# Moving weight copies and accumulating transfers between the stages of an fp32 encoder layer

## The chip, the cores and the metric

The kernel runs on one core of a Trainium2 chip. The core's engines have a queue each: TensorE (PE; its weight loads are listed as PEld), VectorE (DVE), ScalarE (ACT), GpSimd (POOL) and SyncE (SP), which here only issues DMAs. An engine works its queue in order: an instruction that waits holds all behind it. Sixteen DMA engines move the data that SyncE, GpSimd and ScalarE ask for. The metric is the device time of one execution in microseconds, smaller is better.

## The reference

One layer of a streaming encoder, batch 1, 512 positions, width 1024, everything in float32:

```python
hn = rmsnorm(h, norm_mix_g)
fq, fk, fv, ff, gq, gf, gi, gg = split(hn @ w_in)      # 1024 -> 3 x 512 + 8 + 4 x 512
fox_out = forgetting_attention(fq, fk, fv, log_sigmoid(ff + fox_f_bias))   # 8 heads of 64
rec = hgrn2_chunkwise(gq, gf, gi, lbs)                 # 4 heads, state 128 x 128
rec = rmsnorm(rec, hgrn_norm_g) * silu(gg)
h = h + concat([fox_out, rec]) @ w_out                 # 1024 -> 1024
mem_n = rmsnorm(mem, norm_mem_g)                       # 256 memory rows
h = h + cross_attention(rmsnorm(h, norm_x_g), mem_n, w_xq, w_xkv, w_xo)    # 4 heads of 256
u = rmsnorm(h, norm_ff_g) @ w1                         # 1024 -> 4096
h = h + square(relu(u)) @ w2                           # 4096 -> 1024
return rmsnorm(h, final_norm_g)
```

## The kernel before

**Products.** Each float32 operand is split into a high part in a shorter format and the low rest, and each product is made as three matmuls (high by high, high by low, low by high). A weight block comes from memory as a raw tile (`wr`); ScalarE copies it into the high part (`wh`, L181), VectorE subtracts that from the raw tile into the low part (`wl`, L185). The helper `split_of` emits the two.

**Panels.** `specs` lists 38 weight panels of 1 MB in the order of their use: 0 to 12 and 15 from `w_in` (gates, recurrence, the attention's projections), 13, 14 and 16 to 21 from `w_xkv` (values, then keys of the memory), 22 to 25 `w_out`, 26 to 29 `w_xq`, 30 to 33 `w_xo`, 34 to 37 the first two groups of `w1`. `next_panel` hands out a panel and first sees that the one behind it is asked for. `load_next` loads a panel in two halves, a and b (19b is the second half of panel 19), each through `load_unit`: new high and low tiles (four buffers of each, so two panels), a raw tile, the DMAs on SyncE (L205), and the split. Raw tiles come from a pool with two buffers. From panel `LATE` on every third half takes its raw tile from another pool, `t4`, with one buffer, which before that holds the query and key rows (`qk`) of the attention's four projections. `len(stream)` is the number of the panel that is loaded.

**MLP by sums.** The MLP has eight groups of 512 hidden units. For six of the up products and all eight of the down products the 2 x 2 block matrices are multiplied by seven products instead of eight (a Strassen scheme), for which four sums of weight blocks are needed in each case: "5", "7", "6", "4". They are made in memory, ahead of time: `first` copies a block from `w1` or `w2` into a scratch tensor (`wsu` or `wsd`, L433, SyncE, memory to memory, 512 KB), and a later DMA from GpSimd adds another block to it (L443). "6" adds the finished "5" and "4" the finished "6". There are 14 such sets, so 56 copies and 56 accumulations. The deque `copies` holds the copies in pairs of sets (d0 and u2, d1 and u3, and so on; d is down, u is up, the number is the group). In the MLP the sums are loaded as raw tiles (`wrd`, `wru`, L1327) like plain blocks.

**When copies and accumulations are issued.** A copy is issued behind the DMA of a half panel, in program order on SyncE, from panel `COPIES` on, one for each half. An accumulation is issued by `Presum.tick`. Each group of three matmuls reports the time that it should take, and the sum of that, `spent`, is the kernel's own clock; where it passes `self.next`, the next accumulation is emitted and made to wait for the matmul that reported. `PACE` gives the spacing: pairs of a beginning and a gap, and a gap of `None` skips to the next beginning. The clock counts only these matmuls: 183 of it is reached at 271.5 us, 307.2 at 435.6 us.

**Stages and order.** First comes the projection of the gates (panels 0 to 3), then the recurrence over levels 1, 2, 4 to 64 (L797 on TensorE, L803, L822 and L823 on VectorE and GpSimd, mixes on ScalarE), with the projections of panels 4 to 10 filled in between (the class `Fill`). Then come the recurrence's output, and the forgetting attention with panels 10 to 21 as its filling: scores (L1020), softmax (L1031 to L1035), transposes (`pt`, L1043), output (L1059). The stages after it are `w_out`, the cross attention, `w_xo` and the MLP. TensorE's order is that of the program. ScalarE, VectorE, GpSimd and SyncE are ordered by the framework's planner, by its own costs and with priorities (`ahead`), except in a few stretches that are marked as written by hand.

Of the kernel before, what the change touches and what calls it, by code (L numbers as in the profile page):

```python
# [38 lines left out]
NEG = -3.0e38  # L39
SEVEN = (2, 3, 4, 5, 6, 7)  # L40
RAWS, HB, LOADS = 6, 4, 8
COPIES = 3
PACE = (25.0, 9.0), (97.0, None), (183.0, 4.6), (306.0, 9.5)


@with_exitstack
def emit(
# [58 lines left out]
    def t4(name):  # L106
        return t4p.tile([P, D], F32, tag="t4", name=name)
# [25 lines left out]
    def panel(w, n0):  # L133
        return [(slice(0, WT), w[:, n0 : n0 + WT].rearrange("(k p) n -> p k n", p=P))]

    def wide(w, *n0s):

        n = S // len(n0s)
        return [
            [(slice(i * n, (i + 1) * n), w[k0 * P : (k0 + 4) * P, n0 : n0 + n].rearrange("(k p) n -> p k n", p=P)) for i, n0 in enumerate(n0s)]  # L140
            for k0 in (0, 4)
        ]

    specs = []
# [5 lines left out]
    def pair(p):  # L150
        return [
            (slice(0, P), w_in[:, p * P : (p + 1) * P].rearrange("(k p) n -> p k n", p=P)),
            (slice(P, 2 * P), w_in[:, 512 + p * P : 512 + (p + 1) * P].rearrange("(k p) n -> p k n", p=P)),
        ]

    specs += [pair(0), pair(1), panel(w_in, 1024 + WT), pair(2), *wide(w_xkv, D), pair(3), *wide(w_xkv, D + S)]
    for j in range(4):
        specs.append(panel(w_xkv, j * WT))
    LATE = len(specs)
    for w in (w_out, w_xq, w_xo):  # L160
        for j in range(4):
            specs.append(panel(w, j * WT))
# [4 lines left out]
    stream = []  # L167
    state = {"used": 0, "halves": 0}
    copies, copied = deque(), set()
    UW, UK = WT + FH, KC // 2  # L170

    def new_parts(shape, name):
        pad = [P, UK * (UW + FH)]
        hi = whp.tile([P, shape[0] * shape[1]], R, tag="wh", name=f"wh{name}", padded_shape=pad)
        lo = wlp.tile([P, shape[0] * shape[1]], R, tag="wl", name=f"wl{name}", padded_shape=pad)
        return [t.rearrange("p (k n) -> p k n", k=shape[0]) for t in (hi, lo)]

    def split_of(hi, lo, raw):
        def split(what="hl"):
            if "h" in what:  # L180
                ac.activation(hi, raw, AF.Copy)  # L181
            if "v" in what:
                ve.tensor_copy(hi, raw)
            if "l" in what:
                ve.tensor_tensor(lo, raw, f(hi), ALU.subtract)  # L185

        return split

    def load_unit(name, spec, ks, parts=1, between=None):

        nw = max(sl.stop for sl, _ in spec)
        uk = ks.stop - ks.start
        hi, lo = new_parts([uk, nw], name)
        state["halves"] += 1
        if len(stream) >= LATE and state["halves"] % 3 == 0:
            raw_ = t4(f"wr{name}")
        else:
            raw_ = wrp.tile([P, uk * nw], F32, tag="wr", name=f"wr{name}", padded_shape=[P, UK * UW])
        raw_ = raw_.rearrange("p (k n) -> p k n", k=uk)
        nk = uk // parts  # L200
        splits = []
        for q in range(parts):
            qs, src_ks = slice(q * nk, (q + 1) * nk), slice(ks.start + q * nk, ks.start + (q + 1) * nk)
            for sl, src in spec:
                nc.sync.dma_start(raw_[:, qs, sl], src[:, src_ks, :])  # L205
            if between is not None:
                between(q)
            if len(stream) >= COPIES and copies:
                tc.keep_in_program_order(copies.popleft()())
            splits.append(split_of(hi[:, qs, :], lo[:, qs, :], raw_[:, qs, :]))  # L210
        return (hi, lo), splits

    def load_next(parts=2, between=None):

        i = len(stream)
        if i >= len(specs):
            return []
        units, splits = [], []
        uk = specs[i][0][1].shape[1] // 2
        for n in range(2):  # L220
            note = None if between is None else (lambda q, n=n: between(n * parts // 2 + q))
            unit, some = load_unit(f"{i}{'ab'[n]}", specs[i], slice(n * uk, (n + 1) * uk), parts // 2, note)
            units.append(unit)
            splits += some
        stream.append(tuple([u[x] for u in units] for x in range(2)))
        return splits
# [64 lines left out]
    class Fill:  # L291
        def __init__(self):
            self.q = deque()
            self.credit = 0.0
# [152 lines left out]
    class Presum:  # L447
        def __init__(self):
            self.jobs, self.spent, self.next, self.at = deque(), 0.0, PACE[0][0], None

# [12 lines left out]
        def tick(self, us, at):  # L463
            self.spent, self.at = self.spent + us, at
            while self.jobs and self.spent >= self.next:
                gap = next(gap for begin, gap in reversed(PACE) if self.next >= begin)
                if gap is None:
                    self.next = min(begin for begin, _ in PACE if begin > self.next)
                    continue
# [660 lines left out]
    def residual(src_hi, src_lo, g, dst_hi, dst_lo, name, ssq, order, nlast, after=None):  # L1130

        ps_, gens = {}, {}

        def open_(c):
            if c % 2 == 0:
                open_.wt = next_panel()
            ps_[c] = mm(f"{name}{c}")
            gens[c] = gemm_fm(ps_[c], open_.wt, (c % 2) * P, src_hi, src_lo, order=order)

        def early():  # L1140

            for c in range(3):
                open_(c)
                for _ in range(KC - nlast):
                    yield next(gens[c])

        def rest():
            for c in range(KC):
                if c not in gens:
                    open_(c)  # L1150
                yield from gens[c]
                hc = hTc(c)
                ve.tensor_tensor(hc, hc, ps_[c], ALU.add)  # L1153
                ac.activation(dst_hi[:, c, :], hc, AF.Identity, scale=g[:, c : c + 1])  # L1154
                ve.scalar_tensor_tensor(dst_lo[:, c, :], hc, g[:, c : c + 1], f(dst_hi[:, c, :]), op0=ALU.mult, op1=ALU.subtract)
                if ssq is None:
                    pass
                elif c == 0:
                    gp.tensor_tensor(ssq, hc, hc, op=ALU.mult)
                else:  # L1160
                    sq = t2(f"{name}sq{c}")
                    gp.tensor_tensor(sq, hc, hc, op=ALU.mult)
                    gp.tensor_tensor(ssq, ssq, sq, op=ALU.add)
                if after is not None and c in (2, 4, 6):
                    after(c - 2)
                    after(c - 1)

        return early, rest
# [12 lines left out]
    _, wo_rest = residual(mx_hi, mx_lo, g_x, x1_hi, x1_lo, "wo", ssq1, (4, 5, 6, 7, 0, 1, 2, 3), 1)  # L1181
# [539 lines left out]
```

## Time and profile before

| | |
|---|---|
| runs | 760.58, 760.85, 762.68 us; median 760.85 |
| profiled execution | 760.26 us, span 758.1 us |
| TensorE, VectorE, ScalarE, GpSimd busy | 746.6, 537.8, 430.1, 188.6 us |
| moved by DMA | 162.85 MB |
| stages | gates and recurrence to about 161 us, attention and memory keys to 273, `w_out` to 317, cross attention and `w_xo` to 434, MLP to the end |

A row of the timeline gives start, duration, engine, line, operation, what is written and read, and in brackets the engine's idle time before it with what ended that. Buffer numbers are left out of `wrd`, `wsu` and the like. A row of the windows gives a stretch, its length, the busy time of each engine, the granted clock, the share of the 16 DMA engines that was in use and the GB/s. The chain of waits goes back from the last instruction, at each step to what released it. A DMA row in it runs from issue to landing. "DMA to landing" in the view of one tile is the same time.

### The profile page before, as it was taken

Reading aid. Unit: us, or ns where it says so; the run is one execution under the profiler, and the core shown is the slowest. Engines: PE = TensorE matmul, PEld = TensorE weight load, DVE = VectorE, ACT = ScalarE, POOL = GpSimd, SP = SyncE. Lnnn points to the kernel's source line nnn. Section 1 sums busy time; section 2 is a strip of 40 time slices with the busy share of each in tenths; the row PEclk is TensorE's granted clock in tenths of the full one; section 3 lists DMA queues with packets and bytes.
Section 4 is the critical chain, followed back from the end, with each engine's and each line's share of the span. In section 5 each row is a group of like instructions: output and inputs, shape, how many; then the busy total and the mean of one; then the engine's idle time right before and its main releaser. Section 6 shows DMA issues by size and latency. Waiting matters only on the chain.

```text
span 758.1 us, 12049 instructions
## 1 busy us (share of the span) xinstructions
PE 746.6 (98%) x4501; PEld 648.5 (86%) x4501; DVE 537.8 (71%) x844; ACT 430.1 (57%) x715; POOL 188.6 (25%) x274
## 2 busy tenths in 40 slices
PE   9999999999999999999999999999999999999996
PEld 6888878888888888888888888898989999998985
DVE  5646873667877756745555559878788787979697
ACT  5645375556755533334443486657575757575873
POOL 8216552232433227721111110111001100000014
PEclk9999999999999999999999999999999999999999
DMA  7896988455869999997677959697979897847332
GB/s 231 266 250 175 231 213 224 141 156 177 239 249 305 299 282 281 284 280 169 127 170 170 168 114 302 150 297 188 296 185 268 222 271 210 251 151 256 119 113 111
DMA packets 112443, 162.85 MB, mean 215 GB/s; under 512 B 6481, under 2 KB 73594, under 8 KB 112386
## 3 DMA queue, kind: packets, MB, share of 16 engines
q1 hardware_dynamic: 91186, 123.80, 49.8%
q0 software_dynamic: 20608, 37.25, 27.3%
q10 hardware_dynamic: 592, 1.05, 0.4%
q8 instruction: 35, 0.57, 0.3%
q14 instruction: 22, 0.18, 0.1%
HBM read 157.87 MB, written 62.93 MB: 291 GB/s over the span
## 4 chain that ended last, share of the span: by engine, by line
PE 83%; DVE 6%; ACT 4%; DMA 3%; issue 2%; POOL 1%; SPq 0%; ACTq 0%; DVEq 0%; POOLq 0%
PE U L1527 4%; PE U L1526 4%; PE U L1528 4%; PE uU L1401 3%; PE uU L1400 3%; PE uU L1399 3%; PE xq L252 2%; PE wo L252 2%; PE xq L253 2%; PE xq L254 2%; PE xw L252 2%; PE xw L254 2%; PE xw L253 2%; PE wo L253 2%; PE u L254 2%
## 5 line engine op out<-in xcount | busy, mean ns | idle before, releaser
L185 DVE TENSOR_TENSOR wld<-wrd,whd 128x1024 fp32r<-128x1024 f32 x56 | 69.6, 1244 | 17.6 <-ACT whd L181 17.5
L181 ACT ACTIVATE whd<-wrd 128x1024 fp32r<-128x1024 f32 x56 | 59.2, 1058 | 25.1 <-PE uV L1400 8.0
L181 ACT ACTIVATE whu<-wru 128x1024 fp32r<-128x1024 f32 x42 | 44.5, 1059 | 44.9 <-PE uU L1400 18.2
L185 DVE TENSOR_TENSOR wlu<-wru,whu 128x1024 fp32r<-128x1024 f32 x42 | 50.5, 1226 | 14.5 <-ACT whu L181 14.4
L1526 PE MATMUL U<-whd,hb 128*128 128x512 f32 x120 | 46.8, 390 | 0.0
L1527 PE MATMUL U<-wld,hb 128*128 128x512 f32 x120 | 46.8, 390 | 0.0
L1528 PE MATMUL U<-whd,hb 128*128 128x512 f32 x120 | 46.7, 389 | 0.0
L443 POOL DMA_DIRECT2D wsd<-in_w_dram x16 | 16.9, 1053 | 98.0 <-PE U L1528 18.6
L443 POOL DMA_DIRECT2D wsd<-wsd x16 | 14.3, 896 | 95.8 <-PE uU L1401 19.6
L1011 POOL TENSOR_SCALAR bi<-nF,Ft 128x128 f32<-128x128 f32 (+3 forms) x32 | 20.7, 654 | 60.5 <-PE pt L1043 32.8
L1622 POOL TENSOR_TENSOR fa<-acc,gfin 128x512 f32<-128x512 f32 x4 | 6.5, 1654 | 93.0 <-ACT hb L1475 91.2
L443 POOL DMA_DIRECT2D wsu<-in_w_dram x12 | 14.1, 1176 | 59.2 <-PE U L1528 20.3
L1401 PE MATMUL uU<-xs_hi,wlu 128*128 128x256 f32 x96 | 27.2, 283 | 0.0
L1401 PE MATMUL uY<-xs_hi,wlu 128*128 128x256 f32 x96 | 27.2, 283 | 0.0
L1401 PE MATMUL uU<-x_hi,wlu 128*128 128x256 f32 x96 | 27.2, 283 | 0.0
L1399 PE MATMUL uU<-xs_hi,whu 128*128 128x256 f32 x96 | 27.2, 283 | 0.0
L1400 PE MATMUL uU<-x_lo,whu 128*128 128x256 f32 x96 | 27.2, 283 | 0.0
L1400 PE MATMUL uU<-xs_lo,whu 128*128 128x256 f32 x96 | 27.2, 283 | 0.0
L1399 PE MATMUL uY<-xs_hi,whu 128*128 128x256 f32 x96 | 27.2, 283 | 0.0
L1400 PE MATMUL uY<-xs_lo,whu 128*128 128x256 f32 x96 | 27.2, 283 | 0.0
L1399 PE MATMUL uU<-x_hi,whu 128*128 128x256 f32 x96 | 27.2, 283 | 0.0
L1154 ACT ACTIVATE x_hi<-hT,gv 128x512 fp32r<-128x512 f32 x16 | 11.5, 716 | 27.7 <-DVE hT L1153 27.7
(995 smaller groups left out, 2671.6 us busy)
## 6 DMA issues: line engine op xcount, KB each, us to landing
wsd<-in_w_dram SPq DMA_DIRECT2D x32, 512.0 KB, 5.0
wrd<-wsd SPq DMA_DIRECT2D x32, 512.0 KB, 5.4
wsu<-in_w_dram SPq DMA_DIRECT2D x24, 512.0 KB
wrd<-in_w_dram SPq DMA_DIRECT2D x24, 512.0 KB, 5.7
wru<-wsu SPq DMA_DIRECT2D x24, 512.0 KB, 6.4
wru<-in_w_dram SPq DMA_DIRECT2D x18, 512.0 KB, 4.6
wsd<-in_w_dram POOLq DMA_DIRECT2D x16, 512.0 KB, 7.3
wsd<-wsd POOLq DMA_DIRECT2D x16, 512.0 KB, 7.1
```

Of the source, the lines that this page charges most:

```text
L181: ac.activation(hi, raw, AF.Copy)
L185: ve.tensor_tensor(lo, raw, f(hi), ALU.subtract)
L252: te.matmul(ps, wh, hi, start=n_ == 0 and not begun, stop=False)
L253: te.matmul(ps, wh, lo, start=False, stop=False)
L254: at = te.matmul(ps, wl, hi, start=False, stop=k == order[-1])
L443: yield gp.dma_start(wsum[kind, g, name], src, accum_op=ALU.add, **more)
L1399: te.matmul(ps[:, i, :], whi[:, k, ws], xh[:, k, :], start=begin, stop=False, skip_group_check=True)
L1400: te.matmul(ps[:, i, :], whi[:, k, ws], xl[:, k, :], start=False, stop=False, skip_group_check=True)
L1401: at = te.matmul(ps[:, i, :], wlo[:, k, ws], xh[:, k, :], start=False, stop=k == UK - 1, skip_group_check=True)
L1526: te.matmul(ps, hi, whi[:, k, :], start=begin, stop=False, skip_group_check=True)
L1527: te.matmul(ps, hi, wlo[:, k, :], start=False, stop=False, skip_group_check=True)
L1528: at = te.matmul(ps, lo, whi[:, k, :], start=False, stop=k == 1, skip_group_check=True)
```

## The change

```diff
-COPIES = 3
-PACE = (25.0, 9.0), (97.0, None), (183.0, 4.6), (306.0, 9.5)
+COPIES = {7: 2, 16: 1, 17: 0, 21: 1, 29: 2}
+PACE = (183.0, 4.6), (306.0, 6.0), (385.0, 9.0)
...
     specs += [pair(0), pair(1), panel(w_in, 1024 + WT), pair(2), *wide(w_xkv, D), pair(3), *wide(w_xkv, D + S)]
+    LATE = len(specs)
     for j in range(4):
         specs.append(panel(w_xkv, j * WT))
-    LATE = len(specs)
...
-            if len(stream) >= COPIES and copies:
-                tc.keep_in_program_order(copies.popleft()())
+            for _ in range(next((n for at, n in reversed(COPIES.items()) if len(stream) >= at), 0)):
+                if copies:
+                    tc.keep_in_program_order(copies.popleft()())
```

Copies: before, one behind each half of panels 3 to 30. After, none at panels 0 to 6, two behind each half of panels 7 to 15 (36), one at 16 (2), none at 17 to 20, one at 21 to 28 (16), and the last two at the first half of 29.

Accumulations: before, eight from 25 of the kernel's clock at a distance of 9.0, none from 97 to 183, then one every 4.6, and from 306 on every 9.5. After, none ahead of 183, every 4.6 to 306, every 6.0 to 385, every 9.0 from there. Their order stays, so each falls on a later place than before.

Raw tiles: `LATE` goes from 22 to 18, so that halves 19a and 20b take theirs from `t4`, as 22a, 23b and so on do before and after.

## The prediction

> **What bounds the kernel now.** I read the page's busy shares first, then the order of work on TensorE where it sat idle, then the chain of waits back from those places. The page:
>
> ```profile
> span 758.1 us, 12049 instructions
> PE 746.6 (98%) x4501; PEld 648.5 (86%) x4501; DVE 537.8 (71%) x844; ACT 430.1 (57%) x715; POOL 188.6 (25%) x274
> PEclk9999999999999999999999999999999999999999
> ```
>
> TensorE is busy for 98% of the span at full clock, so the kernel can gain only where TensorE pauses. The change alters no matmul. The timeline of TensorE has five pauses of 0.2 us or more after the start (the last number is the idle time, with what ended it):
>
> ```profile
> 61.35 0.36 PE L727 MATMUL dg<-sta,mov 128*64 128x64 f32 x5 [0.85 <-DVE z L694]
> 97.95 0.39 PE L281 MATMUL gg<-wl6b,hn_hi 128*128 128x512 f32 x1
> 98.17 0.39 PE L282 MATMUL gg<-wh6b,hn_lo 128*128 128x512 f32 x1
> 99.74 0.50 PE L280 MATMUL gi<-wh7a,hn_hi 128*128 128x512 f32 x1 [1.18 <-ACT gg L678]
> 166.45 0.30 PE L1043 MATMUL pt<-ident,bi 128*128 128x128 f32 x1 [0.69 <-DVE bi L1035]
> 241.40 0.30 PE L1043 MATMUL pt<-ident,bi 128*128 128x128 f32 x1 [0.21 <-DVE bi L1035]
> 254.64 0.41 PE L1043 MATMUL pt<-ident,bi 128*128 128x128 f32 x2 [0.94 <-DVE bi L1035]
> ```
>
> They add to 0.85 + 1.18 + 0.69 + 0.21 + 0.94 = 3.87 us. A row's length overlaps the next matmul, so each pause costs a little more: from 98.17 to 99.74 is 1.57 us where the row before has 98.17 − 97.95 = 0.22 to the next, a loss of about 1.34 against 1.18 shown. With 0.16 for each of the five the loss is 4.7 us. That is all this change can win. The chain of waits, and ScalarE's timeline, tell what is behind the first and the last two:
>
> ```profile
> 42.40 7.57 DMA wr4b<-in_w_in_dram
> 52.49 5.65 DMA wr5b<-in_w_in_dram
> 59.64 0.89 DVE wl5b L185
> 60.78 0.42 DVE Ac L730
> ...
> 96.64 1.05 ACT wh8a L181
> ...
> 231.86 6.32 DMA wr19a<-in_w_xkv_dram
> 244.17 5.96 DMA wr20b<-in_w_xkv_dram
> ```
> ```profile
> 50.08 1.09 ACT L181 ACTIVATE wh4b<-wr4b 128x1056 fp32r<-128x1056 f32 x1 [4.59 <-DMA wr4b<-in_w_in_dram]
> 58.55 1.06 ACT L181 ACTIVATE wh5b<-wr5b 128x1024 fp32r<-128x1024 f32 x1 [3.88 <-DMA wr5b<-in_w_in_dram]
> 238.20 1.06 ACT L181 ACTIVATE wh19a<-wr19a 128x1024 fp32r<-128x1024 f32 x1 [2.90 <-DMA wr19a<-in_w_xkv_dram]
> 250.21 1.06 ACT L181 ACTIVATE wh20b<-wr20b 128x1024 fp32r<-128x1024 f32 x1 [2.86 <-DMA wr20b<-in_w_xkv_dram]
> ```
>
> No weight is late for its own matmul. A raw half panel is late for its split; the split stands at the head of ScalarE's queue, then of VectorE's, and the small work behind it (Ac at 60.78, the softmax of the attention) comes late to TensorE.
>
> **The change, part by part.** *What a copy costs.* Half panel 11b and the copy right behind it ran alone on the queues:
>
> ```profile
> 131.97 0.56 SPq L433 DMA_DIRECT2D wsu<-in_w_dram  x1
> 131.00:137.00 6.00, 6.00 (x44) 5.50 (x44) 2.77 (x9) 1.04 (x6) 2.08 (x3) 1.00 0.58 175
> ```
>
> A DMA share of 0.58 over 6 us is 3.48 us for two transfers of 512 KB: 1.74 us of all 16 DMA engines each. SyncE needs 0.56 us to issue a copy. There are 56 of them (14 sets of four), before and after.
>
> *No copies at panels 3 to 6, no accumulations at 40 and 50 us.* Load 4b stood behind three copies and shared the engines with the accumulation of 40.32; it took 7.57 us, where one on quiet queues takes 3.7 (half panel 2a; its landing time and the accumulations are in the next fence). So 4b lands about 3.9 us earlier, 5b likewise about 2 us after an issue that itself moves up, since its buffer waits for 4b's split. What is late next is the buffer for 5b's high part, which 3b's matmuls hold:
>
> ```profile
> L253 PE MATMUL gq<-hn_lo,wh3b x8: 389/389/390, 46.9 to 54.4; 128*128 128x512 f32 x8
> DMA to landing us min/median/max: 3.7/3.7/3.7
> 40.32 1.13 POOL L443 DMA_DIRECT2D wsd<-in_w_dram  x1 [11.14 <-PE gq L254]
> 87.55 0.91 POOL L443 DMA_DIRECT2D wsd<-wsd  x1
> 271.53 1.12 POOL L443 DMA_DIRECT2D wsd<-in_w_dram  x1 [1.50 <-PE xk L253]
> 435.60 1.17 POOL L443 DMA_DIRECT2D wsu<-in_w_dram  x1 [3.71 <-PE u L254]
> 643.71 0.88 POOL L443 DMA_DIRECT2D wsd<-wsd  x1 [10.19 <-PE U L1528]
> ```
>
> That ends near 55, so 5b's split moves from 58.55 to about 55, 3.5 us sooner, four times the pause at 61.35. Gain: 0.85 + 0.18 = 1.03 us, bounds 0 and 1.03.
>
> *The eight early accumulations out of the recurrence.* Each holds GpSimd for about 1 us, in order; the one at 87.55 stands before the products that feed the recurrence levels. The pause at 99.74 comes from ScalarE, which from 96.64 runs the split of 8a and then a table load before the activation that frees the PSUM bank. The chain shows no DMA ahead of that, and the levels start when TensorE's own matmuls reach them. GpSimd's 0.91 us can shorten it, a planner that puts the split elsewhere could take all of it: bounds 0 and 1.34, and I take 0.5, nearer the first, because the accumulation at 87.55 lies a level before the pause.
>
> *No copies at panels 17 to 20, third raw tile from panel 18.* 19a and 20b get the tile that so far served the output weights from panel 22, and neither has a copy in front. 6.32 and 5.96 become about 3.7, and the issues move up as well. What is late next is again the high-part buffer: 20b needs that of 18b.
>
> ```profile
> L253 PE MATMUL xk<-mel,wh18b x8: 282/283/284, 240.1 to 245.7; 128*128 128x256 f32 x8
> L181 ACT ACTIVATE wh18b<-wr18b x1: 1061/1061/1061, 232.3 to 232.3; 128x1024 fp32r<-128x1024 f32 x1
> ```
>
> So 20b can be split from about 246 instead of 250.21, 4 us sooner, against pauses of 0.21 and 0.94. Gain (0.21 + 0.16) + (0.94 + 0.16) = 1.47, bounds 0 and 1.47; I take 1.40. The pause at 166.45 has no late load behind it: 0, bounds 0 and 0.85.
>
> *Two copies at each half of panels 7 to 15.* 36 copies where 18 stood; the next load can find 2 × 1.74 = 3.48 us of transfers ahead instead of 1.74. Issue on SyncE grows by 0.56 us a half, under the wait for the buffer. The cover is the time from landing to split; it is thinnest at 15 and 16:
>
> ```profile
> 194.49 0.93 SPq L205 DMA_DIRECT2D wr15b<-in_w_in_dram  x2
> 198.39 0.38 SPq L205 DMA_DIRECT2D wr16a<-in_w_xkv_dram  x1
> 200.17 1.06 ACT L181 ACTIVATE wh15b<-wr15b 128x1024 fp32r<-128x1024 f32 x1 [0.29 <-PE xv L282]
> 204.46 1.04 ACT L181 ACTIVATE wh16a<-wr16a 128x1024 fp32r<-128x1024 f32 x1
> wr25a<-in_w_out_dram SPq DMA_DIRECT2D x1, 512.0 KB, 10.2
> ```
>
> From issue to split there are 5.68 and 6.07 us. A quiet load (3.7) with what is left of the half before, load and two copies, issued 198.39 − 194.49 = 3.90 us earlier (3 × 1.74 − 3.90 = 1.3), takes 5.0. It just fits. If not, the price comes from the holds above: 4.59 + 3.88 + 2.90 + 2.86 = 14.23 us of ScalarE waiting led to 1.03 + 1.47 = 2.50 us lost on TensorE, 0.18 us for each. I take 2 us of new holds, 0.4 us, bounds 0 and the last rival below.
>
> The Trainium skill (DMA: Bandwidth & Descriptors, Queues, rings and completion order) says that each DMA engine takes one ring's descriptors in the order of the ring. By that rule a load on SyncE's queue cannot pass the two copies, and the 1.3 us holds even with nothing else moving; had the copies no such order, the term would be 0 and the sum below 0.4 lower. The 7.57 us of 4b fit the rule but do not prove it.
>
> *The rest.* The pace leaves 27 + 1 accumulations at the places of 271.53 to 435.60, now of the first sums. Then come 13 every 6.0 units of the kernel's own time and 15 every 9.0. A unit is (643.71 − 435.60) / (20 × 9.5) = 1.095 us, so the last goes out at unit 307.2 + 13 × 6.0 + 15 × 9.0 = 520.2, 23 units after 643.71: near 669. Readers:
>
> ```profile
> 454.90 0.35 SPq L1327 DMA_DIRECT2D wrd<-wsd  x1
> 724.59 3.69 SPq L1327 DMA_DIRECT2D wrd<-wsd  x2
> 436.00:521.00 85.00, 85.00 (x459) 73.94 (x459) 66.19 (x78) 58.91 (x86) 9.34 (x12) 1.00 0.79 211
> ```
>
> The first sum is written 180 us before its reader, the last some 55. In 436 to 521 five more accumulations meet a DMA share of 0.79; and TensorE, busy for 85.00 of 85 us, has no pause to lengthen; it would take a load later than its cover. Cost 0.
>
> **Sum**, for the profiled execution of 760.26 us (span 758.1 and 2.16 around it): −1.03 − 0.50 − 1.40 + 0.40 = −2.53, so 757.73. The median of the runs, 760.85, is 0.59 above that execution: 758.3.
>
> **Rivals.** (1) *All five pauses go*, because the planner, which orders ScalarE and VectorE anew, happens to serve 99.74 and 166.45 too: −4.7, 756.1. For it: the bounds above. Against: no load is in those two. (2) *The hold moves to panels 12 to 16.* Halves held by 0.7 us on average over 18 (7a to 15b) are 12.6 × 0.18 = 2.3 us, the gain is given back: 760.6. For it: the thin cover at 15 and 16. Against: with the accumulations gone, the queues carry little else there. (3) *The loads were not the cause*: the small work stays where the planner put it, behind splits that now wait for buffers: 760.9. Against: the buffers are free 3 to 4 us before the splits ran. (4) *Slower: the loads fall behind.* There are two raw buffers; with a load of L us and a split of 1.06 on ScalarE and about as long again on VectorE, a half comes every (L + 2.3) / 2. The splits of 15b and 16a stand 204.46 − 200.17 = 4.29 us apart, and a split runs 240.1 − 232.3 = 7.8 us ahead of its first matmul (18b). If two copies push L to the 10.2 us of 25a, the eight halves 13a to 16b lose 8 × (6.25 − 4.29) = 15.7 us, 7.9 more than the cover: 760.85 − 2.93 + 7.9 = 765.8. It decides from L = 9 us on, where 8 × (5.65 − 4.29) − 7.8 = 3.1 eats the gain. For it: 25a's 10.2 is this kernel's, with one copy on each half. Against: 25a had an accumulation every (435.60 − 271.53) / 27 = 6.1 us beside it, and 13a to 16b have none.
>
> **Chances.** Forecast 0.50, with a range of its own of 757.3 to 759.3; rival 1 0.12, rival 2 0.17, rival 3 0.08, rival 4 0.13. A difference under 0.3% (2.28 us) cannot be told from none, so faster ends at 758.57: of the forecast 0.42 lies below it and 0.08 above. Faster 0.42 + 0.12 = 0.54, same 0.08 + 0.17 + 0.08 = 0.33, slower 0.13. The range goes from rival 1 to past rivals 2 and 3, 756.0 to 762.0; rival 4 is left out.
>
> **What would show it.** Right: no pause before the dg matmuls and before the transposes near 241 and 254, no ScalarE wait on a load at 4b, 5b, 19a, 20b, and loads of 15b and 16a under 6 us. Wrong: a new pause of TensorE between 130 and 230 behind a split that waits for its load (rivals 2 and 4), the same pauses with no load behind them (3), or any pause after 271, which would mean that a sum or its reader came late.

## The result, and the profile after

Six runs of each kernel on one chip: after 756.83 us (755.97 to 757.91), before 761.41 us (760.12 to 762.75). The ratio is 0.9939, with a 95% interval of 0.9924 to 0.9955: the change saves 4.6 us, between 3.4 and 5.8. The profiled execution of after took 756.48 us, 3.78 less than that of before.

The page of after, its head and TensorE's busy row. The count of matmuls is that of before, and so is the busy time within 0.5 us:

```profile
span 754.5 us, 12053 instructions
PE 746.1 (99%) x4501; PEld 648.9 (86%) x4501; DVE 537.4 (71%) x844; ACT 431.1 (57%) x715; POOL 190.3 (25%) x274
```

TensorE's timeline of after, at the five matmuls that stood behind a pause before:

```profile
60.67 0.64 PE L728 MATMUL dg<-sta,mov 128*64 128x64 f32 x16
...
97.66 0.39 PE L281 MATMUL gi<-wh7a,hn_hi 128*128 128x512 f32 x1
...
164.24 0.30 PE L1044 MATMUL pt<-ident,bi 128*128 128x128 f32 x1 [0.69 <-DVE bi L1036]
...
238.82 1.04 PE L1044 MATMUL pt<-ident,bi 128*128 128x128 f32 x8
...
250.94 0.60 PE L1044 MATMUL pt<-ident,bi 128*128 128x128 f32 x4
```

Four of the five rows have lost their bracket; only the pause at 164.24 stays, with its 0.69 us. The starts also tell what each was worth, since the order of TensorE is the same in both kernels. Against 61.35, 99.74, 241.40 and 254.64 these rows come 0.68, 2.08, 2.58 and 3.70 us sooner. The start of the kernel, which the change does not touch, ran 0.34 us later in this execution: that is the distance of each matmul from its counterpart between 12 us and the first pause. Taken from the matmul just ahead of each pause to the few behind it, the pauses gave 1.06, 1.46, 0.40 and 1.13 us, 4.05 in all. Between the pauses the distance does not change by more than 0.05 us. Less the 0.34 that is the 3.70 us by which the last matmul comes sooner, and the 3.6 us by which the span fell, up to the tail. Nothing was lost elsewhere.

ScalarE's timeline of after, the splits that the prediction followed, and two of the doubled copies' stage:

```profile
46.57 1.09 ACT L181 ACTIVATE wh4b<-wr4b 128x1056 fp32r<-128x1056 f32 x1 [0.74 <-DMA wr4b<-in_w_in_dram]
55.48 1.06 ACT L181 ACTIVATE wh5b<-wr5b 128x1024 fp32r<-128x1024 f32 x1 [2.02 <-PE gq L255]
...
202.57 1.06 ACT L181 ACTIVATE wh16a<-wr16a 128x1024 fp32r<-128x1024 f32 x1 [0.22 <-DMA wr16a<-in_w_xkv_dram]
...
205.67 1.06 ACT L181 ACTIVATE wh16b<-wr16b 128x1024 fp32r<-128x1024 f32 x1 [0.49 <-DMA wr16b<-in_w_xkv_dram]
...
231.30 1.06 ACT L181 ACTIVATE wh19a<-wr19a 128x1024 fp32r<-128x1024 f32 x1 [0.54 <-PE xv L283]
...
243.50 1.06 ACT L181 ACTIVATE wh20b<-wr20b 128x1024 fp32r<-128x1024 f32 x1 [0.38 <-PE xk L254]
```

4b waits 0.74 us for its load instead of 4.59. 5b, 19a and 20b wait for no load any more but for a high-part buffer that TensorE still reads, and are split 3.07, 6.90 and 6.71 us sooner than before. At 16a and 16b the doubled copies do hold ScalarE, for 0.22 and 0.49 us, where before has no wait, and no pause of TensorE follows.

The pause at 99.74 has no load in it. It was made on GpSimd and VectorE, a level or two ahead. First the timelines of before (VectorE, GpSimd and ScalarE), then the same work in after:

```profile
77.16 1.20 POOL L443 DMA_DIRECT2D wsu<-in_w_dram  x1
77.82 1.98 POOL L825 TENSOR_TENSOR F<-F 128x256 f32<-128x256 f32 x2
78.66 1.20 DVE L745 SCALAR_TENSOR_TENSOR lf<-z,za 128x32 f32<-128x32 f32 x1
...
80.39 0.42 DVE L823 TENSOR_TENSOR sta<-sta,F 128x256 f32<-128x256 f32 x1
...
88.14 1.93 DVE L822 TENSOR_TENSOR sta<-sta,F 128x256 f32<-128x256 f32 x1
88.15 1.62 POOL L823 TENSOR_TENSOR mov<-mov,F 128x256 f32<-128x256 f32 x2
...
99.00 1.26 ACT L678 ACTIVATE gg<-gg,r 128x512 f32<-128x512 f32 x2
```
```profile
77.68 0.41 DVE L824 TENSOR_TENSOR sta<-sta,F 128x256 f32<-128x256 f32 x1
...
79.47 0.18 DVE L746 SCALAR_TENSOR_TENSOR lf<-z,za 128x32 f32<-128x32 f32 x1
...
85.47 0.41 DVE L823 TENSOR_TENSOR sta<-sta,F 128x256 f32<-128x256 f32 x1
87.14 2.28 POOL L824 TENSOR_TENSOR mov<-mov,F 128x256 f32<-128x256 f32 x2 [2.21 <-PE lv L798]
...
94.81 1.26 ACT L679 ACTIVATE gg<-gg,r 128x512 f32<-128x512 f32 x2
```

Before, an accumulation stood on GpSimd at 77.16 ahead of the product `F`, and one at 87.55 ahead of the product `mov`. Twice a row of VectorE then falls beside that product and lasts until GpSimd is through: `lf` takes 1.20 us instead of 0.18 and ends at 79.86 (GpSimd at 79.80), `sta` 1.93 instead of 0.41 and ends at 90.07 (GpSimd at 89.77).

Two things bring them together. VectorE's order differs: before, `lf` and what hangs on it stand ahead of the level's first `sta`, in after behind the last. With that and the long `lf` the first `sta` comes at 80.39 instead of 77.68. So the last `sta` is late as well and runs into `mov`, while in after it is through (at 85.88) when `mov` begins at 87.14. The accumulation at 87.55 adds less: `mov` begins 1.11 us after TensorE starts the product `lv` that it waits for, in after 0.84.

The activation that frees TensorE's bank comes at 99.00 instead of 94.81. Of that 4.19 us only 0.68 was there already at 61.35; 1.5 is the long `sta` and about 2 the level with `lf`, of which 1.0 is the long `lf` itself. The early `lf` stands in the traces of before, e3 and e6 below, which have an accumulation near 77 us, and these three alone have the pause near 99. No run has the one order without the accumulation or the other with it, so how much is the planner's order and how much the meeting of the two engines is not shown. The Trainium skill (SBUF — State Buffer, Who interferes with whom) says that a VectorE instruction with two inputs in SBUF and a GpSimd instruction that reads SBUF need the same port, and that whichever starts second waits until the other is done. The ends of these two rows agree with it, within 0.3 us; which of the two began first they do not tell, since `sta` and `mov` start 0.01 us apart.

### The profile page after: what moved, and what is told of

It reads as the page before. It is cut to its first block, busy times and chain, and to the rows that moved or that the text cites. A ratio compares the mean times of both kernels' runs of the same rounds, so it can differ in the third digit from the quotient of the medians.

```text
span 754.5 us, 12053 instructions
## 1 busy us (share of the span) xinstructions
PE 746.1 (99%) x4501; PEld 648.9 (86%) x4501; DVE 537.4 (71%) x844; ACT 431.1 (57%) x715; POOL 190.3 (25%) x274
## 3 DMA queue, kind: packets, MB, share of 16 engines
q10 hardware_dynamic: 592, 1.05, 0.4%
## 4 chain that ended last, share of the span: by engine, by line
PE 95%; DVE 1%; ACT 1%; POOL 1%; issue 1%; ACTq 0%; POOLq 0%
PE U L1528 4%; PE U L1527 4%; PE U L1529 4%; PE uU L1402 3%; PE uU L1401 3%; PE uU L1400 3%; PE xq L253 2%; PE wo L253 2%; PE xq L254 2%; PE xw L253 2%; PE xq L255 2%; PE xw L255 2%; PE u L255 2%; PE xw L254 2%; PE wo L255 2%; PE u L254 2%
## 5 line engine op out<-in xcount | busy, mean ns | idle before, releaser
L1529 PEld LDWEIGHTS U<-whd,hb 128*128 128x128 f32 x120 | 22.5, 188 | 4.7
```

What stands on the lines that cost most here:

```text
L1529: at = te.matmul(ps, lo, whi[:, k, :], start=False, stop=k == 1, skip_group_check=True)
```

## The experiments

Twelve kernels. "Before" is the kernel before, run on the same chip as the kernel of that row. The ratio and its interval stand as recorded; they need not be the quotient of the two medians.

| label | median us (range, runs) | before | ratio, 95% interval | profiled execution |
|---|---|---|---|---|
| e1_pace | 757.88 (756.59 to 760.12, 10) | 760.77 | 0.9963, 0.9950 to 0.9976 | 759.66 |
| e3_late | 761.74 (759.43 to 767.46, 10) | 760.77 | 1.0005, 0.9981 to 1.0030 | 761.47 |
| e4_copies_3to6 | 756.22 (755.84 to 756.39, 4) | 760.77 | 0.9945, 0.9930 to 0.9960 | 756.28 |
| e5_copies_17to20 | 757.36 (756.45 to 758.73; 6, one of them 4254.54) | 760.77 | 0.9954, 0.9935 to 0.9973 | 758.73 |
| e2_no_late | 758.61 (757.92 to 762.15, 9) | 760.98 | 0.9967, 0.9950 to 0.9985 | 760.55 |
| e6_acc_77_124 | 757.50 (756.81 to 760.28, 10) | 760.98 | 0.9954, 0.9939 to 0.9969 | 760.12 |
| e8_acc_40_50 | 757.04 (756.85 to 757.23, 4) | 760.98 | 0.9933, 0.9910 to 0.9956 | 757.23 |
| e7_stress_13to16 | 768.45 (768.34 to 768.62, 4) | 760.98 | 1.0084, 1.0064 to 1.0103 | 768.34 |
| e9_fill | 756.84 (756.66 to 757.51, 6) | 761.69 | 0.9930, 0.9907 to 0.9952 | 756.71 |
| e10_dense | 756.60 (756.40 to 761.39, 9) | 761.69 | 0.9943, 0.9921 to 0.9965 | 756.92 |
| e11_fill_3to6 | 757.34 (756.70 to 757.88, 6) | 761.69 | 0.9932, 0.9907 to 0.9957 | 757.88 |
| e12_shift | 755.18 (755.00 to 755.43, 6) | 760.82 | 0.9924, 0.9903 to 0.9944 | 755.00 |

The profiled executions of e1, e2, e5 and e6 lie 1.4 to 2.6 us above their medians. What their traces show is so in that execution; by the medians it costs less.

**Accumulations alone (e1_pace).** The kernel before with only the new pace:

```diff
-PACE = (25.0, 9.0), (97.0, None), (183.0, 4.6), (306.0, 9.5)
+PACE = (183.0, 4.6), (306.0, 6.0), (385.0, 9.0)
```

> The kernel before with the new pacing alone: no accumulation ahead of 271 us, copies and raw tiles as before. If GpSimd's accumulations at 77 and 87 us stretch the recurrence levels, the pause at 99.74 (1.18 us) is gone, while the one near 61 (0.85) stays at half or more, since load 4b still stands behind three copies, and those near 241 and 254 (0.21, 0.94) stay: span 1.3 us shorter than 758.1, so about 756.8. If the traffic of the accumulations at 40 and 50 us is what makes 4b late, the pause near 61 goes too and the span is about 755.8. If the pause at 99 hangs on the planner's order of ScalarE alone, it stays and the span is about 758.

Its timelines, TensorE and ScalarE:

```profile
61.15 0.64 PE L727 MATMUL dg<-sta,mov 128*64 128x64 f32 x16
...
98.14 0.39 PE L280 MATMUL gi<-wh7a,hn_hi 128*128 128x512 f32 x1
...
254.38 0.63 PE L1043 MATMUL pt<-ident,bi 128*128 128x128 f32 x4 [2.43 <-DVE bi L1035]
...
249.95 1.06 ACT L181 ACTIVATE wh20b<-wr20b 128x1024 fp32r<-128x1024 f32 x1 [4.35 <-DMA wr20b<-in_w_xkv_dram]
```

The pauses at 61 and at 99 are both gone, though a copy stands behind every half from panel 3 on. Those at 241 and 254 stay, and the last has grown from 0.94 to 2.43 us, so that this execution is hardly shorter than that of before; 20b's split waits 4.35 us for its load. So the first two are the accumulations', the last two are not.

**The third raw tile alone (e3_late).** The kernel before with only the move of `LATE`:

```diff
+    LATE = len(specs)
     for j in range(4):
         specs.append(panel(w_xkv, j * WT))
-    LATE = len(specs)
```

> The kernel before with the third raw tile from panel 18 alone, copies and pacing as before. If the copies at panels 17 to 20 make 19a and 20b late, the pauses near 241 and 254 (0.21 and 0.94 us) keep half or more of their 1.15 us, since 19a and 20b are still queued behind copies: span 757.3 to 758.1. If it is the raw tile that makes them late, both pauses are gone: span about 756.6. The pauses near 61, 99 and 166 stay in either case.

TensorE's timeline of it:

```profile
242.94 0.63 PE L1043 MATMUL pt<-ident,bi 128*128 128x128 f32 x4 [0.92 <-DVE bi L1035]
```

The pause at 254 is gone; that at 241 has grown from 0.21 to 0.92 us, and one of 0.56 us stands right behind it, at 244.14. With the copies still between the loads, a third tile moves the pause by a panel. No gain in the time. The pause near 61 takes 1.35 us in this trace, against 0.85, though nothing ahead of panel 18 was changed: by so much a pause behind late loads can differ from one execution to the next.

**All but the raw tile (e2_no_late).** The kernel after with `LATE` back at 22 (the same three lines, reversed).

> The changed kernel without the third raw tile at panels 18 to 21 (it starts at 22 again). If taking the copies away from 17 to 20 was enough, the waits of ScalarE for 19a and 20b stay under 2 us and there is no pause near 241 and 254: span within 0.4 us of 754.5. If the third tile is needed as well, 19a and 20b are issued only when the split before has freed a buffer (231 us or later for 19a), ScalarE waits 2 us or more and a pause of 0.4 us or more comes back near 241 or 254: span 0.4 to 1.2 us above 754.5.

SyncE's queue, ScalarE and TensorE:

```profile
226.92 0.37 SPq L205 DMA_DIRECT2D wr22a<-in_w_out_dram  x1
227.34 1.07 SPq L434 DMA_DIRECT2D wsd<-in_w_dram  x1
229.63 0.37 SPq L205 DMA_DIRECT2D wr19a<-in_w_xkv_dram  x1
...
238.10 1.06 ACT L181 ACTIVATE wh19a<-wr19a 128x1024 fp32r<-128x1024 f32 x1 [5.01 <-DMA wr19a<-in_w_xkv_dram]
...
241.29 0.93 PE L1044 MATMUL pt<-ident,bi 128*128 128x128 f32 x4 [2.31 <-DVE bi L1036]
```

The free tile of `t4` goes to 22a, six halves ahead of its turn, and a copy goes with it. 19a, needed first, is asked for behind both and is split 8.5 us after its issue. In after the tile serves 19a at once, asked for at 226.9 and split at 231.30. TensorE loses 4.1 us here, of which 1.6 are half clock behind the pause (last section). The stretch without copies is therefore worth little without the tile: against before, the pace alone saves 2.9 us, pace and copies without the tile 2.4, all three 4.6. The tile alone saved nothing (e3); what it saves next to the other two parts, without the stretch, is e5's question. The copies alone were not tried: the early accumulations would have added to blocks that are not there yet.

**One copy at panels 3 to 6 again (e4_copies_3to6).** The kernel after with

```diff
-COPIES = {7: 2, 16: 1, 17: 0, 21: 1, 29: 2}
+COPIES = {3: 1, 7: 2, 16: 1, 17: 0, 21: 1}
```

> The changed kernel with one copy again behind each half of panels 3 to 6 (the later ones run out sooner). If these copies make 4b and 5b late, ScalarE waits 3 to 4 us again for each and the pause near 61 is back with 0.5 to 0.9 us: span 0.6 to 1.0 us above 754.5. If the accumulations were the cause, no pause near 61 and a span within 0.3 us of 754.5.

ScalarE's timeline:

```profile
48.00 1.09 ACT L181 ACTIVATE wh4b<-wr4b 128x1056 fp32r<-128x1056 f32 x1 [2.19 <-DMA wr4b<-in_w_in_dram]
...
56.01 1.06 ACT L181 ACTIVATE wh5b<-wr5b 128x1024 fp32r<-128x1024 f32 x1 [2.57 <-PE dg L728]
```

4b is 1.4 us later than in after, 5b 0.5, and no pause of TensorE follows near 61: copies there cost nothing. The expectation that they make the pause failed, and with it half of my reason for the first term.

**One copy at panels 17 to 20 again (e5_copies_17to20).** The kernel after with

```diff
-COPIES = {7: 2, 16: 1, 17: 0, 21: 1, 29: 2}
+COPIES = {7: 2, 16: 1}
```

> The changed kernel with one copy again behind each half of panels 17 to 20, the third raw tile from 18 kept. If the copies are the cause of the pauses near 241 and 254, at least half of their 1.15 us is back: span 0.6 to 1.5 us above 754.5. If the raw tile alone removed them, no pause near 241 and 254: span within 0.3 us of 754.5.

ScalarE's and TensorE's timelines:

```profile
235.58 1.06 ACT L181 ACTIVATE wh19a<-wr19a 128x1024 fp32r<-128x1024 f32 x1 [3.38 <-DMA wr19a<-in_w_xkv_dram]
...
240.32 0.63 PE L1044 MATMUL pt<-ident,bi 128*128 128x128 f32 x4 [1.82 <-DVE bi L1036]
```

The pause of 241 is back, a second one of 0.56 us follows at 241.52, and the span is 2.2 us longer than that of after (756.7 against 754.5). But this execution is the slowest of five; three of them took 756.45 to 756.58. Without the one of 4254.54 us, whose cause is not known, the median is 756.58, 0.4 us over e4's of the same chip. So a copy ahead of weights that come just in time can cost 2 us; in most runs here it cost a few tenths.

**Early accumulations again, at two places (e6_acc_77_124 and e8_acc_40_50).** The kernel after with five accumulations from 76 us on, and with those of 40 and 50 us; the copies that they need go ahead of them:

```diff
-COPIES = {7: 2, 16: 1, 17: 0, 21: 1, 29: 2}
-PACE = (183.0, 4.6), (306.0, 6.0), (385.0, 9.0)
+COPIES = {6: 2, 16: 1, 17: 0, 21: 1, 29: 2}
+PACE = (52.0, 9.0), (97.0, None), (183.0, 4.6), (306.0, 6.0), (385.0, 9.0)
```
```diff
-COPIES = {7: 2, 16: 1, 17: 0, 21: 1, 29: 2}
-PACE = (183.0, 4.6), (306.0, 6.0), (385.0, 9.0)
+COPIES = {3: 1, 4: 0, 7: 2, 16: 1, 17: 0, 21: 1, 29: 2}
+PACE = (25.0, 9.0), (43.0, None), (183.0, 4.6), (306.0, 6.0), (385.0, 9.0)
```

> The changed kernel with five accumulations at the clock's 52, 61, 70, 79 and 88 again (about 77, 87, 102, 111 and 124 us) and the copies that they need two panels' halves earlier, behind 6a and 6b, which have 10 us of cover. If accumulations on GpSimd stretch the levels of the recurrence, the pause before the second projection of the gates (99.74 in the kernel before, 1.18 us) is back with 0.6 us or more, with no load late: span 0.8 to 1.6 us above 754.5. If the planner's order of ScalarE was the cause, or the earlier start of the levels after the pause at 61 went, there is none: span within 0.4 us of 754.5.

> The changed kernel with two accumulations at the clock's 25 and 34 again (about 40 and 50 us) and the two copies that they need behind 3a and 3b; no copies at panels 4 to 6. If the accumulations make 4b and 5b late, ScalarE waits 2 us or more for 4b and the pause near 61 is back with 0.4 to 0.9 us: span 0.4 to 1.2 us above 754.5. If it takes copies and accumulations together, 4b is split by 48.5, 5b waits for its buffer only, and there is no pause: span within 0.4 us of 754.5.

e6, GpSimd, VectorE and TensorE, then e8, ScalarE and TensorE:

```profile
86.57 1.16 POOL L444 DMA_DIRECT2D wsu<-in_w_dram  x1
87.25 1.79 POOL L824 TENSOR_TENSOR mov<-mov,F 128x256 f32<-128x256 f32 x2
87.17 2.17 DVE L823 TENSOR_TENSOR sta<-sta,F 128x256 f32<-128x256 f32 x1
...
99.51 0.50 PE L281 MATMUL gi<-wh7a,hn_hi 128*128 128x512 f32 x1 [1.92 <-ACT gg L679]
```
```profile
49.73 1.09 ACT L181 ACTIVATE wh4b<-wr4b 128x1056 fp32r<-128x1056 f32 x1 [3.80 <-DMA wr4b<-in_w_in_dram]
...
58.50 1.06 ACT L181 ACTIVATE wh5b<-wr5b 128x1024 fp32r<-128x1024 f32 x1 [4.17 <-DMA wr5b<-in_w_in_dram]
61.30 0.69 PE L728 MATMUL dg<-sta,mov 128*64 128x64 f32 x16 [0.35 <-DVE z L695]
```

Each brings back one pause and not the other. In e6 no load is late; `lf` stands ahead of `sta` again and takes 1.20 us, and the last `sta` meets `mov` and grows to 2.17 us, as in before. The pause costs 2.2 us in the starts, and the half clock behind it (last section) another 1.6. In e8 both loads are late again by as much as before, and TensorE's pause is 0.35 us, 0.57 in the starts: about half of the 1.06 that the change took away. By the medians e6 stays 0.5 us over e8 on the same chip, with ranges that meet, so e6's price in an ordinary run is not settled; the place of the pause is.

**Loads that do fall behind (e7_stress_13to16).** The kernel after with one copy at 7 to 12 and four at each half of 13 to 16:

```diff
-COPIES = {7: 2, 16: 1, 17: 0, 21: 1, 29: 2}
+COPIES = {7: 1, 13: 4, 17: 0, 21: 1, 29: 2}
```

> The changed kernel with one copy behind each half of panels 7 to 12 and four behind each of 13 to 16 (7 us of transfers where two made 3.5). By the price of 0.18 us of TensorE for each us that ScalarE waits for a load, eight halves held by 2 to 3.5 us cost 3 to 5 us, in pauses before the transposes of the attention: span 757.5 to 759.5. If the loads fall behind as a whole (one half in 6.3 us against 4.3 that the splits need), matmuls of panels 15 to 18 wait for their own weights as well: span 762 or more. If the cover is larger than I read it, no pause of 0.5 us between 170 and 230: span under 755.5.

TensorE's and ScalarE's timelines:

```profile
203.97 0.63 PE L1044 MATMUL pt<-ident,bi 128*128 128x128 f32 x4 [4.11 <-DVE bi L1036]
232.12 0.50 PE L282 MATMUL xv<-wl16b,meh 128*128 128x512 f32 x1 [0.64 <-DVE wl16b L185]
...
219.24 1.06 ACT L181 ACTIVATE wh16a<-wr16a 128x1024 fp32r<-128x1024 f32 x1 [3.09 <-DMA wr16a<-in_w_xkv_dram]
```
16a is asked for at 206.6 and split 12.6 us later, and the span is 11.9 us longer than that of after. Of this 3.1 us are two stretches of half clock behind the pauses (last section). Even a weight's own matmul is late (232.12). This is the last rival's mechanism, at four copies instead of two.

**Accumulations close together in the MLP (e10_dense).** The kernel after with all 56 at the same spacing:

```diff
-PACE = (183.0, 4.6), (306.0, 6.0), (385.0, 9.0)
+PACE = ((183.0, 4.6),)
```

> The kernel after with all 56 accumulations every 4.6 units of the kernel's clock, so that the 28 from 436 us on stand every 5 us instead of every 6.6 to 9.9 us and are through at about 577 us instead of 669. The theory that the MLP's accumulations cost nothing while TensorE has no pause there: no pause after 271 us, span 754.5 us within 0.5, time 756.8 within 0.6. The rival, that five or more of them beside a DMA share near 0.8 push loads past their cover: pauses of TensorE between 436 and 577 us, and a span 1 us or more longer.

The windows view of after and then of e10, 436 to 521 us:

```profile
436.00:521.00 85.00, 85.00 (x459) 73.88 (x457) 66.20 (x79) 61.19 (x88) 13.16 (x16) 1.00 0.95 241
```
```profile
436.00:521.00 85.00, 85.00 (x460) 73.92 (x458) 66.17 (x80) 61.27 (x88) 17.49 (x20) 1.00 1.05 257
```

The DMA engines' share rises from 0.79 in before to 0.95 and 1.05, and TensorE is busy for all of the 85 us in each. (A packet's whole time counts in the stretch in which it starts, so the share can pass 1.) Nothing to pay in the MLP, even so, in this trace and in the seven runs up to 756.98 us. Two of the nine took 760.93 and 761.39, at the lowest mean clocks of the nine; they left no trace, and why they were slow is open.

**The pause that was left (e9_fill, e11_fill_3to6, e12_shift).** In after TensorE reaches the attention's first transposes before VectorE has the weights. `FX` says how much filling goes between the scores and the next transposes, by row tile:

```diff
-FX = (4.4, 4.4, 5.4, 5.4), (3.3, 3.9, 4.5, 5.1)
+FX = (5.4, 4.4, 5.4, 5.4), (3.3, 3.9, 4.5, 5.1)
```

That is e9, and e11 with the copies of e4. e12 has

```diff
-FX = (4.4, 4.4, 5.4, 5.4), (3.3, 3.9, 4.5, 5.1)
+FX = (5.4, 4.4, 4.4, 5.4), (3.3, 3.9, 4.5, 5.1)
```

> The kernel after with one unit (about 1 us) more of filling between the first scores and the first transposes of the attention, where TensorE still pauses for 0.69 us because VectorE has the normalised weights only 0.9 us after TensorE gets there. The theory that only VectorE's queue is late there, and that no load is behind it: the pause at 164 us goes, TensorE's last matmul ends 0.85 us sooner, profiled span about 753.7 us, time about 756.0. The rival, that the planner orders VectorE by the filling and the softmax comes later by as much: the pause stays at about 0.7 us and the span at 754.5.

> e9's filling with one copy behind each half of panels 3 to 6 and none at 29. Copies at 3 to 6 cost nothing by the run that tried them alone, so the time is e9's: 753.7 us of span, about 756.0 us; by the theory that two copies at each half of 7 to 15 are covered in any case, nothing is gained by 8 copies fewer before 21 either. The rival, that loads 15a to 16b still hold small work a little in the kernel after: e11 is 0.3 us or more under e9.

> e9 with the unit of filling that it gave to the first transposes taken back from those of the third row tile, where in the kernel after VectorE has the weights 2.7 us before TensorE comes for them (bi ends at 176.33, pt starts at 179.05). e9's new pause of 0.94 us at 268.85 us, at the end of the attention, comes by this theory from filling that ran out there by the one unit; so neither pause stands: span about 753.6 us (754.5 less 0.85), time about 755.9. The rival, that the pause at 268.85 comes from another order of VectorE's work and not from filling: it stays near 0.9 us and the span is again 754.5 to 754.7.

TensorE's timeline of e9 at the end of the attention, then of e12 at the first transposes:

```profile
268.85 1.09 PE L1060 MATMUL pv<-pts,fv 128*64 128x128 f32 x14 [0.94 <-DVE pts L1050]
```
```profile
163.79 0.38 PE L1044 MATMUL pt<-ident,bi 128*128 128x128 f32 x2
```

e9 only moves the pause: filling given to the first row tile is missing at the end of the attention, and the time is that of after. e11 has the same pause there and is no faster than e9 (757.34 against 756.84), so eight copies taken from panels 26 to 29 and put at panels 3 to 6 gain nothing. e12 takes the unit from the third row tile, where the weights are ready early, and neither pause is left: TensorE has none of 0.2 us or more after the start. The profiled span is 753.0 us, 1.5 less than that of after, of which 0.4 comes from a start that happened to run sooner. At 755.18 us, with no run above 755.43, e12 lies under all runs of after, the lowest of which took 755.97. But the two were not run side by side, and the intervals of their ratios to before overlap.

## Why the prediction was right, and where not

The prediction of 758.3 us was 1.5 us too high. The time lies within its range, below the forecast's own 757.3 and nearer to rival 1's 756.1: the direction and most places were right, two sizes were not. The sizes found are those of the two traced executions.

- **Pause at 61.35: 1.03 predicted, 1.06 found.** 5b's split went to 55.48 with the buffer late next, as forecast ("near 55"). The reason was half wrong. I named the copies and the accumulations together; e1 and e4 leave the copies in and lose nothing, e8 brings the accumulations back with two copies and half of the pause returns.
- **Pause at 99.74: 0.50 predicted, 1.46 found.** This is the step that failed, as a size: I took "nearer the first", GpSimd's 0.91 us, out of bounds of 0 and 1.34, because "the accumulation at 87.55 lies a level before the pause". The delay does not stay on GpSimd: with the accumulations comes another order on VectorE and a meeting of the two engines, and VectorE's single rows then cost 1.02 and 1.52 us more. e1 and e6 show from both sides that the accumulations make the pause. Rival 1 gave this pause to the planner; in so far as its order of VectorE is behind it, that was right too. The two long rows stood in the trace of before, the `sta` among others of its form with 0.41 us. What the pause costs in an ordinary run is less sure: by the medians e6, which has it, is 0.7 us over after (757.50 against 756.83, not run side by side).
- **Pauses at 241.40 and 254.64: 1.40 predicted, 1.53 found.** The mechanism held, with the buffers late next at 19a and 20b. That it takes both, the tile and the free stretch, to be rid of the pauses was not foreseen: e2, e3 and e5 each lack one of the two, and the traces of all three keep a pause of 0.9 us or more near 241.
- **Pause at 166.45: 0, and 0 found.** VectorE's queue makes it, no load. e12 took it away with filling.
- **New holds at 15 and 16: 0.40 predicted, 0 found.** The loads were slower than the 5.0 us that I worked out: 16a took 6.3 from issue to landing by its tile view, so my sign of being right, loads of 15b and 16a under 6 us, did not come at 16a. ScalarE was held all the same for only 0.71 us at 16a and 16b. And the price, "0.18 us for each", has the wrong form: holds cost nothing until the small work behind them is late. e4 is held 2.19 us by the load of 4b and has no pause there, before was held 4.59 + 3.88 and lost 1.06; in e7 the seven holds from 14b to 18a, 18.8 us together, go with 11.9 us of span, 3.1 of it half clock.
- **Accumulations in the MLP: 0, and 0 found**, in e10's trace too.

Of the 1.2 us by which the trace beats the sum (3.70 against 2.53) 0.96 is the pause at 99.74, 0.40 the holds that did not come, 0.16 the other pauses, and −0.34 the start. The rest of the 1.5 lies between the profiled executions and the medians: I added 0.59 to the one, and after's median is 0.35 over its own.

Rivals 2 and 3 fell: no pause moved to panels 12 to 16, and the splits did move with the loads. Rival 4 did not come at two copies; e7 shows that it was no idle fear. By its own sum loads of 12.6 us would lose 8 × (7.45 − 4.29) − 7.8 = 17.5 us, and e7 lost 11.9, of which 3.1 are half clock.

## What to carry to other kernels

Put background transfers behind loads that have slack, and count that slack to the first consumer of the work queued behind the split, not to the split. Before you price a DMA issue on GpSimd by its own row, look what stands behind it in the queue, whether VectorE will be working at that moment, and whether VectorE's order changes with it. When the last pauses are short, move filling from a place with slack instead of adding it: what is added at one place is missing at another.

## What the runs showed of the hardware that was not expected

TensorE's clock can halve for one stretch of 3.41 us, by a fixed grid: from the first step to full clock to the first halving it is 95.57 us in e6, 235.52 in e2 and 197.97 in e7, which is 28, 69 and 58 stretches. The windows view of e6, of e7 and of e1, cut at the clock's own steps (the second number in the row is the length, the third TensorE's busy time; the clock is third from the end):

```profile
96.87:100.28 3.41, 1.49 (x7) 0.93 (x6) 2.79 (x8) 3.38 (x5) 0.33 (x2) 1.00 0.71 237
100.28:103.70 3.42, 3.42 (x9) 2.63 (x8) 1.75 (x5) 3.37 (x8) 2.47 (x4) 0.50 1.02 306
```
```profile
198.31:201.72 3.41, 1.55 (x7) 0.94 (x5) 0.76 (x3) 0.67 (x1) 0.11 (x1) 1.00 1.08 364
201.72:205.13 3.41, 1.16 (x8) 1.19 (x9) 2.41 (x7) 1.75 (x6) 0.65 (x1) 1.00 1.05 332
205.13:208.54 3.41, 3.41 (x9) 2.69 (x9) 2.16 (x8) 1.51 (x5) 2.83 (x7) 0.50 1.04 341
```
```profile
252.82:256.23 3.41, 1.85 (x14) 1.88 (x15) 3.14 (x9) 2.30 (x6) 1.33 (x1) 1.00 0.83 260
256.23:259.65 3.42, 3.42 (x31) 3.42 (x30) 3.22 (x9) 2.73 (x6) 1.49 (x4) 1.00 0.83 278
```

In e6 a pause of 1.92 us lies within one stretch, TensorE is busy for 1.49 us of it, and the next stretch runs at 0.50. In e7 a stretch with 1.55 busy is followed by full clock, one with 1.16 by half. In e1 a longer pause, 2.43 us, falls on two stretches, the second has 1.85 busy (the first more), and nothing happens. e2 (1.10 busy) and e7's second pause (1.49) were followed by half clock too. Here, then, the step lies between 1.49 and 1.55 us of work in a stretch of 3.41. Each of the four halved stretches cost 1.6 us against the starts in after, nearly as much as a pause.

Where the grid lies differs from execution to execution: its first step comes 4.0 to 7.3 us after the start of the span in the traces, so the same pause can fall within one stretch or on two. This may be a part of why these kernels scatter by two or three us from run to run, and the clocks on record fit it. One halved stretch takes 0.002 off a run's mean clock. In e6 the two runs at 0.996, one of which is the profiled one, took 760.12 and 760.28 us; the eight at 0.998 or 0.999 took 756.81 to 757.91. That gap is wider than the 1.6 us of one stretch, so it is not the whole cause; the runs without a trace leave the rest open.

The Trainium skill (TensorE: Matmul & The Clock Gate, What's actually happening) tells of a free-running window of 3413 ns. The traces agree with its length. The Trainium skill, on the same page (Why this matters for your kernels), asks for no idle gaps over some 3 us; here 1.92 was enough where it fell within one window, and 2.43 was not where it fell on two.
